# A down projection with seven block products in place of eight in six of its 16 pairs of feature blocks

## The chip, the cores and the metric

One core of one Trainium2 chip runs the whole program in one launch. The metric is the device time of that launch in microseconds (us). An execution counts from its first to its last instruction (the span) and a small remainder around it.

## The reference

The program is a trunk of two layers on 256 tokens of 2048 features, all in float32. Each layer has a token mixer (a retention layer first, block-sparse attention second), a squared-ReLU MLP with 8192 inner features, and a gated embedding. Cut to what matters here:

```python
def rms_norm(x, g):
    y = x * lax.rsqrt(jnp.mean(x * x, axis=-1, keepdims=True) + RMS_EPS)
    return y * g

def sq_relu_mlp(xn, w_up, w_down):
    return jnp.square(jax.nn.relu(xn @ w_up)) @ w_down

for i in range(DEPTH):                       # DEPTH = 2
    h = h + (retention(...) if i == 0 else moba_attention(...))
    h = h + sq_relu_mlp(rms_norm(h, mlp_norm_g[i]), mlp_w_up[i], mlp_w_down[i])
    h = h + per_layer_embed(h, p[i], ...)
return rms_norm(h, final_norm_g)
```

## The kernel before

**Units and pairs.** Every weight matrix is cut on the host into units of 128 partitions x 1024 columns. Two units form a pair of 1 MB, which one transfer of the SP queue brings into a tile `raw` (three buffers). A float32 weight is not multiplied as it is. `conv(i)` splits unit i into a high part `wh` (a rounding cast on ACT, line 221) and a low part `wl` (the rest, `raw - wh`, a subtraction on DVE, line 222), both in the type fp32r, and a product of two split numbers is three matmuls: high x high, high x low, low x high.

**Order.** There is no scheduler; each engine executes its instructions as `run` writes them. For each unit i it issues the load of the pair three pairs ahead, the split of unit i+3 (`LOOK = 3`, four buffers of `wh` and of `wl`), the matmuls of unit i, and then the small tasks that were registered for i with `at(i, ...)`: evacuations of PSUM, norms, transposes. ACT and DVE so run a fixed number of units ahead of PE, and a buffer of `wh` is free for the next split when PE has done with the unit in it.

**The MLP** goes in two halves of 4096 inner features. In an up projection (`phase_a`, names `up0_`, `up1_`) the weights stand still and the 256 tokens of both parts move: a unit is eight matmuls of 512 columns and eight of 256, and two units make a tile of 128 inner features. `evac_up` adds the two halves of the bank (`fold`: a copy `t` on ACT at line 226, an add on DVE at line 227), squares with ReLU (`s2`, line 533) and, one unit later, splits the result into `act[n]` (named `a`). The norm's factor of a token is not in `act`. It comes in at the end, squared, as `r2`, one number for each token.

In a down projection (`project` and `phase_b`, names `dn`) the activations stand still, 128 features x 128 tokens, and 512 weight columns move. For each of four groups of 512 output columns, `c`, the 16 units of a half are gone through; a unit holds two blocks of 128 features and is twelve matmuls, 2 blocks x 2 halves of the tokens x 3. They gather in two of the four PSUM banks of the name `mm`, so that the next group begins in the other two. `evac_dn` adds them, times `r2`, to the residual `h` (line 542). After the second half `finish` squares `h`, transposes it and prepares the operands of what follows. The other banks are two named `y` and two named `aux`.

Of the kernel before, what the change touches and what calls it, by code (L numbers as in the profile page):

```python
# [46 lines left out]
def pack(units):  # L47
    u = units.reshape(-1, 2, P, UC).transpose(0, 2, 1, 3)
    return u
# [10 lines left out]
def cut_b(w):  # L60
    k, n = w.shape
    u = w.reshape(k // 256, 2, P, n // 512, 512).transpose(3, 0, 2, 1, 4)
    return u.reshape(-1, P, UC)


def cut_d(w):
    u = w.reshape(4, 4, P, 2, 2, P).transpose(0, 3, 2, 4, 1, 5)
    return u.reshape(-1, P, UC)


class Core:
    def __init__(self, nc, tc, pools, io):
        self.nc, self.tc, self.io = nc, tc, io
        self.cp, self.wp, self.sp, self.pp = pools
        self.units, self.tasks = [], {}
        self.raws, self.ready = {}, {}


    def unit(self, src, j, mm):
        self.units.append((src, j, mm))  # L80
        return len(self.units) - 1

    def at(self, i, fn):
        self.tasks.setdefault(i, []).append(fn)

    def load(self, i):
        if i >= len(self.units):
            return
        src, j, _ = self.units[i]
        if j % 2:  # L90
            return
        t = self.wp.tile([P, 2, UC], F32, name=f"raw{i}", tag="raw", bufs=3)
        self.nc.sync.dma_start(t, self.io[src][j // 2])
        self.raws[i] = self.raws[i + 1] = t

    def conv(self, i):
        if i >= len(self.units):
            return
        raw = self.raws.pop(i)[:, self.units[i][1] % 2, :]
        wh = self.wp.tile([P, UC], F32R, name=f"wh{i}", tag="wh", bufs=LOOK + 1)  # L100
        wl = self.wp.tile([P, UC], F32R, name=f"wl{i}", tag="wl", bufs=LOOK + 1)
        self.split(wh, wl, raw)
        self.ready[i] = (wh, wl)

    def run(self):
        for fn in self.tasks.pop(-1, []):
            fn()
        for i in range(2, LOOK):
            self.conv(i)
# [29 lines left out]
        return self.sp.tile(list(shape), dt, name=name, tag="s")  # L139

    def small(self, name):
        return self.wp.tile([P, S], F32, name=name, tag="small", bufs=6)


    def mm_a(self, ps, wh, wl, rhs, first, last, turned=False):
# [144 lines left out]
    def stats_b(self):  # L290

        ps = self.aux("rb")
        for t in range(2):
            self.nc.tensor.matmul(ps[:, t * P:(t + 1) * P], self.rn[:, t:t + 1].to_broadcast([P, P]), self.ident, start=True, stop=True)
        self.rb = self.cp.tile([P, S], F32, name="rb", tag="rb", bufs=2)
        self.nc.scalar.copy(self.rb, ps[:, :S])


    def start(self):
        nc, cp, io = self.nc, self.cp, self.io  # L300
        self.g = cp.tile([P, 8, KD], F32, name="g")
        nc.scalar.dma_start(self.g, io["gains"])
        warm = cp.tile([P, 2], F32, name="warm")
        nc.vector.memset(warm, 0.0)
        nc.scalar.activation(warm, warm, AF.Silu)
        self.warm(WARM)
        self.h = [cp.tile([P, 2, 512], F32, name=f"h{c}") for c in range(KD // 4)]
        self.xt = [self.slot("xt", (P, 2, S)) for _ in range(KD // 2)]
        self.raws[0] = self.raws[1] = raw = self.wp.tile([P, 2, UC], F32, name="raw0", tag="raw", bufs=3)
# [12 lines left out]
        load_x(3)  # L322
        self.raws[2] = self.raws[3] = raw2 = self.wp.tile([P, 2, UC], F32, name="raw2", tag="raw", bufs=3)
        for v in range(2):
            dma(raw2[:, v], io["ret_in"][1][:, v])
        load_x(4)
        load_x(5)
        self.load(4)
        load_x(6)
        load_x(7)  # L330
        self.ident = cp.tile([P, P], F32, name="ident")
        dma(self.ident, io["ident"])
        self.cs = cp.tile([P, 2, S], F32, name="cs")
        dma(self.cs, io["cs"])
        self.xx = {}
        wh = self.wp.tile([P, UC], F32R, name="wh0", tag="wh", bufs=LOOK + 1)
        wl = self.wp.tile([P, UC], F32R, name="wl0", tag="wl", bufs=LOOK + 1)
        for n in range(2):
            self.start_x(n)
        for c in (slice(0, 256), slice(256, 512)):  # L340
            self.split(wh[:, c], wl[:, c], raw[:, 0, c])
            if c.start == 0:
                for n in range(2, 4):
                    self.start_x(n)
        self.split(wh[:, 512:], wl[:, 512:], raw[:, 0, 512:])
        self.ready[0] = (wh, wl)
        wh = self.wp.tile([P, UC], F32R, name="wh1", tag="wh", bufs=LOOK + 1)
        wl = self.wp.tile([P, UC], F32R, name="wl1", tag="wl", bufs=LOOK + 1)
        for c in (slice(0, 512), slice(512, 1024)):
            self.split(wh[:, c], wl[:, c], self.raws.pop(1, raw)[:, 1, c])  # L350
        self.ready[1] = (wh, wl)
        for n in range(4, 8):
            self.start_x(n)
# [153 lines left out]
    def natural(self, banks, r):  # L507
# [7 lines left out]
            lo.append(b)  # L515
        return hi, lo

    def mlp(self, layer, gains):
        nc = self.nc
        st = {}  # L520

        def scales():
            self.stats_a()
            st["r2"] = self.cp.tile([P, 2], F32, name="r2", tag="r2", bufs=2)
            nc.vector.tensor_mul(st["r2"], self.rn, self.rn)
        self.at(len(self.units) + 4, scales)
        act = {}
        for half in range(2):
            def evac_up(n, ps, half=half):
                t = self.small("t")  # L530
                self.fold(t, ps)
                s = self.small("s2")
                nc.vector.scalar_tensor_tensor(s, t, 0.0, t, op0=ALU.max, op1=ALU.mult)  # L533
                act[n] = self.slot(f"a{n}", dt=F32R)
                yield
# [3 lines left out]
            def evac_dn(c, banks, i, half=half):  # L539
                for t in range(2):  # L540
                    h = self.h[c][:, t]
                    nc.vector.scalar_tensor_tensor(h, banks[t], st["r2"][:, t:t + 1], h, op0=ALU.mult, op1=ALU.add)  # L542
                if half:
                    self.finish(c, i, gains)
# [53 lines left out]
    def last(self, st, src):  # L598


        nc = self.nc
        per, hold = KD // 2, LOOK + 1
        b = len(self.units)
        fin = {"ssq": {}}

# [214 lines left out]
def program(nc, io):  # L820
    with tile.TileContext(nc) as tc, tc.manual_schedule(), \
            tc.tile_pool(name="const", bufs=1) as cp, tc.tile_pool(name="w", bufs=1) as wp, \
            tc.tile_pool(name="slots", bufs=59) as sp, \
# [12 lines left out]
        c.ple(1, [G_FIN])  # L836
        c.run()
# [63 lines left out]
```

## Time and profile before

| | us |
|---|---|
| median of 3 runs | 2758.9 (2758.51 to 2759.28) |
| span of the profiled execution | 2756.9 |
| PE busy with matmuls | 2743.4 of 2756.9 |
| DVE busy | 1694.6 |
| ACT busy | 1322.8 |

The profiled execution's own time is not listed apart from the three runs; its span is 2.0 us below their median, which is what lies around the span. A busy share is a mean over the program: whether an engine that is at 61% holds up another is read in the stretch in question, from the waits. In the rows, `x4` behind a group is a count, a bracket tells how long the engine had been idle and what ended that, and tile names stand as output`<-`inputs.

### The profile page before, as it was taken

How to read it: one execution, taken by the hardware profiler on the slowest of the kernel's cores; microseconds unless marked ns; L12 is line 12 of the kernel's file. 1: busy time of each engine (PE TensorE's matmuls, PEld its weight loads, DVE VectorE, ACT ScalarE, POOL GpSimd, SP SyncE). 2: the span in 40 equal slices, each digit the busy share in tenths (PEclk: the TensorE clock that was granted, in tenths of full speed). 3: DMA queues.
4: the chain of work that ended last, by engine and by line, in shares of the span. 5: the costliest groups of instructions: out<-in, count | busy, mean ns of one | idle time of the engine just before them, and what ended most of it. 6: DMA issues, size and time to landing. Idle time of an engine off the chain costs nothing.

```text
span 2756.9 us, 34160 instructions
## 1 busy us (share of the span) xinstructions
PE 2743.4 (100%) x13744; PEld 2334.7 (85%) x13744; DVE 1694.6 (61%) x2321; ACT 1322.8 (48%) x1844; POOL 0.2 (0%) x4
## 2 busy tenths in 40 slices
PE   9999999999999999999999999999999999999998
PEld 7888888888888888888888888888888888888886
DVE  6766666655576544665546777775666446664555
ACT  6444444444454433454445555554544334544454
POOL 0000000000000000000000000000000000000000
PEclk9999999999999999999999999999999999999999
DMA  7455555555555555555565555555555555555554
GB/s 277 177 186 186 186 186 186 186 183 186 185 195 186 196 194 190 192 188 192 186 204 188 185 182 179 182 178 185 187 190 192 195 188 196 185 193 189 186 199 153
DMA packets 79450, 522.48 MB, mean 190 GB/s; under 512 B 8987, under 2 KB 12988, under 8 KB 17596
## 3 DMA queue, kind: packets, MB, share of 16 engines
q1 hardware_dynamic: 78476, 519.20, 53.1%
q10 hardware_dynamic: 816, 1.11, 0.3%
q8 instruction: 107, 1.75, 0.3%
q14 instruction: 51, 0.42, 0.0%
HBM read 517.39 MB, written 2.88 MB: 189 GB/s over the span
## 4 chain that ended last, share of the span: by engine, by line
PE 98%; DMA 1%; DVE 0%; ACT 0%; issue 0%; SPq 0%; ACTq 0%; DVEq 0%
PE up L155 17%; PE up L153 9%; PE qk L155 4%; PE aq L155 2%; PE ak L155 2%; PE qk L153 2%; PE aq L153 1%; PE ak L153 1%; PE pu L573 1%; DMA raw<-ret_in 1%; PE xt L255 1%; PE y L461 1%; PE dn__11046 L195 0%; PE dn__20748 L196 0%; PE dn__21353 L197 0%; PE dn__11358 L196 0%
## 5 line engine op out<-in xcount | busy, mean ns | idle before, releaser
L222 DVE TENSOR_TENSOR wl<-raw,wh 128x1024 fp32r<-128x1024 f32 (+1 forms) x971 | 1180.0, 1221 | 652.7 <-ACT wh L221 639.2
L221 ACT CAST wh<-raw 128x1024 fp32r<-128x1024 f32 (+1 forms) x971 | 1013.5, 1048 | 709.3 <-DVE rs_y L278 29.2
L155 PE MATMUL up<-x,wh 128*128 128x512 f32 x2048 | 490.5, 391 | 0.0
L155 PEld LDWEIGHTS up<-x,wh 128*128 128x128 f32 x2048 | 376.1, 188 | 72.4
L153 PEld LDWEIGHTS up<-x,wl 128*128 128x128 f32 x2048 | 263.4, 191 | 10.4
L153 PE MATMUL up<-x,wl 128*128 128x256 f32 x2048 | 266.7, 283 | 0.0
L226 ACT COPY t<-up 128x256 f32<-128x256 f32 x128 | 47.6, 372 | 331.6 <-PE up L155 331.6
L227 DVE TENSOR_TENSOR t<-t,up 128x256 f32<-128x256 f32 x128 | 53.9, 421 | 216.7 <-ACT t L226 216.5
L155 PE MATMUL qk<-x,wh 128*128 128x512 f32 x448 | 109.9, 393 | 0.0
L155 PEld LDWEIGHTS qk<-x,wh 128*128 128x128 f32 x448 | 81.8, 188 | 15.5
L233 ACT ACTIVATE x<-xt,g 128x256 fp32r<-128x256 f32 x112 | 52.5, 478 | 50.6 <-DVE x L234 39.4
L234 DVE SCALAR_TENSOR_TENSOR x<-xt,g,x 128x256 fp32r<-128x256 f32 x112 | 53.0, 481 | 25.7 <-ACT x L233 25.5
L155 PE MATMUL aq<-x,wh 128*128 128x512 f32 x256 | 63.3, 392 | 0.0
L155 PE MATMUL ak<-x,wh 128*128 128x512 f32 x256 | 62.9, 392 | 0.0
L153 PEld LDWEIGHTS qk<-x,wl 128*128 128x128 f32 x448 | 57.4, 191 | 2.2
L153 PE MATMUL qk<-x,wl 128*128 128x256 f32 x448 | 58.1, 283 | 0.0
L533 DVE SCALAR_TENSOR_TENSOR s<-t 128x256 f32<-128x256 f32 x128 | 54.4, 425 | 4.4
L155 PEld LDWEIGHTS ak<-x,wh 128*128 128x128 f32 x256 | 46.7, 189 | 8.7
L155 PEld LDWEIGHTS aq<-x,wh 128*128 128x128 f32 x256 | 46.5, 189 | 8.7
L222 DVE TENSOR_TENSOR a<-s,a 128x256 fp32r<-128x256 f32 x128 | 53.6, 419 | 0.0
L221 ACT CAST a<-s 128x256 fp32r<-128x256 f32 x128 | 52.0, 406 | 0.0
L242 ACT ACTIVATE sq<-h 128x512 f32<-128x512 f32 x48 | 30.1, 628 | 37.5 <-DVE h L542 15.6
(895 smaller groups left out, 4999.3 us busy)
## 6 DMA issues: line engine op xcount, KB each, us to landing
raw<-mlp_up SPq DMA_DIRECT2D x128, 1024.0 KB, 4.8
raw<-mlp_dn SPq DMA_DIRECT2D x128, 1024.0 KB, 4.8
raw<-ret_in SPq DMA_DIRECT2D x94, 1024.0 KB, 4.8
raw<-att SPq DMA_DIRECT2D x48, 1024.0 KB, 4.8
raw<-ret_out SPq DMA_DIRECT2D x32, 1024.0 KB, 4.8
raw<-ple_gate SPq DMA_DIRECT2D x32, 1024.0 KB, 4.8
raw<-att_o SPq DMA_DIRECT2D x16, 1024.0 KB, 4.8
raw<-ple_up SPq DMA_DIRECT2D x4, 1024.0 KB, 4.8
```

Source lines behind the costliest of these rows:

```text
L153: mm(ps[:, S:], wl[:, c], rhs[k][:, :S], start=False, stop=end)
L155: mm(ps, wh[:, c], rhs[k], start=first and k == 0, stop=end)
L221: self.nc.scalar.copy(dst_h, src)
L222: self.nc.vector.tensor_sub(dst_l, src, dst_h.bitcast(F32))
L226: self.nc.scalar.copy(dst, ps[:, :S])
L227: self.nc.vector.tensor_add(dst, dst, ps[:, S:])
L233: self.nc.scalar.activation(t[:, :S], src, AF.Copy, scale=gs)
L234: self.nc.vector.scalar_tensor_tensor(t[:, S:], src, gs, t[:, :S].bitcast(F32), op0=ALU.mult, op1=ALU.subtract)
L242: self.nc.scalar.activation(self.slot("sq"), self.h[c][:, t], AF.Square, accum_out=self.ssq[:, t, c:c + 1])
L255: self.nc.tensor.transpose(ps[:, o * P:(o + 1) * P], self.h[c][:, t, f * P:(f + 1) * P], self.ident)
L461: mm(ys[t], a, w, start=i == 0, stop=i == len(ops) - 1)
L533: nc.vector.scalar_tensor_tensor(s, t, 0.0, t, op0=ALU.max, op1=ALU.mult)
```

## The change

Take a pair of feature blocks a, b of the down projection, the two halves of the tokens, and two groups of 512 output columns. The activations are then a 2 x 2 table of blocks, the weights another, and their product takes eight block products of three matmuls each. The change computes it in seven (Winograd's form of Strassen's method) for the pairs q = 2, 4, 7, 9, 12 and 14 of each 16 (`FAST`), called quick pairs below; the other ten stay as eight products, called plain. It does so in three of the four quarters of each layer's down projection; in the last quarter (second half, last two column groups) `phase_b` stays.

- `sweep` replaces `phase_b` there. It goes through the 16 pairs of a half once for 1024 output columns. The results for 2 token halves x 2 column groups gather in all four `mm` banks, `C00` to `C11`, and the common products of the quick pairs in `P1`, `P5` (the `y` banks) and `P6`, `P7` (the `aux` banks). A plain pair is two units of twelve matmuls. A quick pair is four units, called L, C, M and X here: `low` (6 matmuls), `corner` (3, on 512 columns), `mixed` (6) and `crossed` (6).
- For M and X, DVE first forms differences of weight blocks in place in `raw`, two subtractions of 512 columns each (lines 583, 584, 589 and 590), and then the unit is split as always.
- `combine` forms four sums and differences of the two activation blocks of a quick pair (lines 621 to 624, 128 columns each) and splits them; 24 times in all.
- Since activations of different tokens are now added, the factor `r2` has to be in them: `spread` turns it into rows (two small matmuls and a copy) and `evac_up` multiplies each tile with it (line 638, 128 times). The final add to `h` then has no factor.
- After a sweep `done` adds the four C banks to `h`; one unit later `first` and two units later `second` add the P banks in eight further steps.
- `LOOK` is 4, with five buffers of `wh` and `wl`; during the first twelve units of the program the split still runs three ahead (`SOON`). `raw` keeps three buffers; a load is issued at a pair's first unit. There are 62 slots for 59 and 8 small tiles for 6.

```diff
-LOOK = 3
+LOOK = 4
+SOON = 3
+HOLD = 4
+FAST = [q in (2, 4, 7, 9, 12, 14) for q in range(16)]
...
     def run(self):
...
         for i in range(len(self.units)):
-            self.load(i + 6)
-            self.conv(i + LOOK)
+            self.load(self.units[i][0] + 3)
+            while done <= i + (SOON if i < 12 else LOOK):
+                self.conv(done)
+                done += 1
             wh, wl = self.ready.pop(i)
             self.units[i][2](wh, wl)
...
+    def sweep(self, name, src, first, fast, x, done):
...
+            if quick:
+                plan += [(q, self.low, [("C01", (q, "S4"), 0), ("C00", (b, 0), 1)]),
+                         (q, self.corner, [("P1", (a, 0), 0)]),
+                         (q, self.mixed, [("P5", (q, "S1"), 0), ("P7", (q, "S3"), 1)]),
+                         (q, self.crossed, [("P6", (q, "S2"), 0), ("C10", (b, 1), 1)])]
+            else:
+                plan += [(q, lambda raw: self.halves(raw[:, 0]), plain(a, False)),
+                         (q, lambda raw: self.halves(raw[:, 1]), plain(b, True))]
...
+    def mixed(self, raw):
+        v, r = self.nc.vector, raw[:, 0]
+        v.tensor_sub(r[:, :512], r[:, 512:], r[:, :512])
+        v.tensor_sub(r[:, 512:], raw[:, 1, :512], r[:, 512:])
+        return self.halves(r)
+
+    def crossed(self, raw):
+        v, r = self.nc.vector, raw[:, 1]
+        v.tensor_sub(r[:, :512], r[:, :512], raw[:, 0, :512])
+        v.tensor_sub(r[:, 512:], r[:, 512:], r[:, :512])
+        return self.halves(r)
...
+        def combine(q, a, b):
...
+            v.tensor_add(s1, a[:, P:], b[:, P:])
+            v.tensor_sub(s2, s1, a[:, :P])
+            v.tensor_sub(s3, a[:, :P], a[:, P:])
+            v.tensor_sub(s4, b[:, :P], s2)
+            self.split(h, l, f)
...
+                v.tensor_mul(s, s, st["rb"])
                 self.split(act[n][:, :S], act[n][:, S:], s)
+                if FAST[n // 2]:
...
+            def done(banks, i, g, half=half):
+                h = [self.h[2 * g], self.h[2 * g + 1]]
+                for bank in ("C00", "C10", "C01", "C11"):
+                    t, c = int(bank[1]), int(bank[2])
+                    v.tensor_add(h[c][:, t], h[c][:, t], banks[bank])
...
+                self.at(i + 1, first)
+                self.at(i + 2, second)
...
-            self.project(f"dn{half}_", f"mlp_dn{layer}", half * 64, FH // 256, lambda k: act[k], evac_dn)
+            for g in range(2):
+                if half and g:
+                    for c in (2, 3):
+                        e = len(self.units) + n - 1
+                        self.phase_b(f"dn{c}_", src, (4 + c) * n, n, lambda k: act[k], lambda banks, c=c, e=e: evac_dn(c, banks, e))
+                else:
+                    self.sweep(f"dn{half}{g}_", src, (half * 2 + g) * n, FAST, x, lambda banks, i, g=g, done=done: done(banks, i, g))
```

What stands on DVE for the first pairs of the first down projection, before: one subtraction of 1024 columns for each unit, two for each tile `raw`.

```order
L222 TENSOR_TENSOR wl326_7776<-raw326_7719,wh326_7775 128x1024
L222 TENSOR_TENSOR wl327_7794<-raw326_7719,wh327_7793 128x1024
L222 TENSOR_TENSOR wl328_7810<-raw328_7757,wh328_7809 128x1024
L222 TENSOR_TENSOR wl329_7828<-raw328_7757,wh329_7827 128x1024
L222 TENSOR_TENSOR wl330_7844<-raw330_7791,wh330_7843 128x1024
L222 TENSOR_TENSOR wl331_7862<-raw330_7791,wh331_7861 128x1024
```

The same engine in the changed kernel, at the quick pair q = 4 of that projection (`raw164`) and the first unit of the plain pair behind it:

```order
L238 TENSOR_TENSOR wl_7913<-raw164_7854,wh_7912 128x1024
L238 TENSOR_TENSOR wl_7925<-raw164_7854,wh_7924 128x512
L583 TENSOR_TENSOR raw164_7854<-raw164_7854 128x512
L584 TENSOR_TENSOR raw164_7854<-raw164_7854 128x512
L238 TENSOR_TENSOR wl_7940<-raw164_7854,wh_7939 128x1024
L589 TENSOR_TENSOR raw164_7854<-raw164_7854 128x512
L590 TENSOR_TENSOR raw164_7854<-raw164_7854 128x512
L238 TENSOR_TENSOR wl_7958<-raw164_7854,wh_7957 128x1024
L238 TENSOR_TENSOR wl_7976<-raw165_7892,wh_7975 128x1024
```

A quick pair has eight rows where a pair had two, and the splits of M and X stand behind the differences from which they are made.

Where a group of columns ends in the first down projection, DVE had this before (`dn0_0_0`, `dn0_0_1` are its two banks; the next group was by then in two others):

```order
L222 TENSOR_TENSOR wl337_7964<-raw336_7893,wh337_7963 128x1024
L222 TENSOR_TENSOR wl338_7980<-raw338_7927,wh338_7979 128x1024
L542 SCALAR_TENSOR_TENSOR h0_89<-dn0_0_0__7725,r2_6197,h0_89 128x512
L542 SCALAR_TENSOR_TENSOR h0_89<-dn0_0_1__7726,r2_6197,h0_89 128x512
L222 TENSOR_TENSOR wl339_8000<-raw338_7927,wh339_7999 128x1024
```

At the end of the first sweep it now has this (`raw177` is the second pair of the next sweep, `raw178` its first quick pair):

```order
L238 TENSOR_TENSOR wl_8391<-raw177_8349,wh_8390 128x1024
L238 TENSOR_TENSOR wl_8407<-raw177_8349,wh_8406 128x1024
L651 TENSOR_TENSOR h0_89<-h0_89,dn00_C00__7819 128x512
L651 TENSOR_TENSOR h0_89<-h0_89,dn00_C10__7823 128x512
L651 TENSOR_TENSOR h1_90<-h1_90,dn00_C01__7827 128x512
L651 TENSOR_TENSOR h1_90<-h1_90,dn00_C11__7831 128x512
L238 TENSOR_TENSOR wl_8429<-raw178_8388,wh_8428 128x1024
L657 TENSOR_TENSOR h0_89<-h0_89,q_8448 128x512
L658 TENSOR_TENSOR q_8448<-q_8448,dn00_P6__7928 128x512
L659 TENSOR_TENSOR u_8449<-q_8448,dn00_P5__7916 128x512
L238 TENSOR_TENSOR wl_8455<-raw178_8388,wh_8454 128x512
```

All four C banks, in which the next sweep begins at once, are emptied behind the split of a pair two pairs ahead, and the P banks between the splits of the next quick pair.

More of the change, by code (lines that the diff above doesn't have):

```diff
@@ L74, in __init__, with part @@
         self.cp, self.wp, self.sp, self.pp = pools
-        self.units, self.tasks = [], {}
+        self.units, self.pairs, self.tasks = [], [], {}
         self.raws, self.ready = {}, {}
     def unit(self, src, j, mm):
-        self.units.append((src, j, mm))
+        return self.part(src, j // 2, lambda raw: self.halves(raw[:, j % 2]), mm)
+    def part(self, src, pair, conv, mm):
+        if not self.pairs or self.pairs[-1] != (src, pair):
+            self.pairs.append((src, pair))
+        self.units.append((len(self.pairs) - 1, conv, mm))
         return len(self.units) - 1
@@ L84, in at, with load, operand, halves @@
         self.tasks.setdefault(i, []).append(fn)
-    def load(self, i):
-        if i >= len(self.units):
+    def load(self, q):
+        if q >= len(self.pairs) or q in self.raws:
             return
[L89 to L94, printed above, removed]
-    def conv(self, i):
[L97 to L103, printed above, removed]
+        src, pair = self.pairs[q]
+        t = self.raws[q] = self.wp.tile([P, 2, UC], F32, name=f"raw{q}", tag="raw", bufs=3)
+        self.nc.sync.dma_start(t, self.io[src][pair])
+    def operand(self, cols=UC):
+        return [self.wp.tile([P, cols], F32R, name=f"w{n}", tag=f"w{n}", bufs=LOOK + 1) for n in "hl"]
+    def halves(self, raw):
+        wh, wl = self.operand(raw.shape[-1])
+        self.split(wh, wl, raw)
+        return wh, wl
+    def conv(self, i):
+        if i < len(self.units):
+            q, conv, _ = self.units[i]
+            self.ready[i] = conv(self.raws[q])
     def run(self):
@@ L516, in natural, with plain, mm @@
         return hi, lo
+    def sweep(self, name, src, first, fast, x, done):
+        plan, banks, seen = [], {}, {}
+        tags = {"P1": "y", "P5": "y", "P6": "aux", "P7": "aux"}
+        cut = (slice(0, 512), slice(512, 1024))
+        def plain(k, second):
+            cols = (1, 0) if second else (0, 1)
+            order = (1, 0) if second else (0, 1)
+            return [(f"C{t}{cols[j]}", (k, t), j) for j in order for t in range(2)]
+        for q, quick in enumerate(fast):
+            a, b = 2 * q, 2 * q + 1
+            if quick:
[6 more added lines that the diff above has]
+                         (q, lambda raw: self.halves(raw[:, 1]), plain(b, True))]
+        for n, (_, _, ops) in enumerate(plan):
+            for m, (bank, _, _) in enumerate(ops):
+                seen.setdefault(bank, []).append((n, m))
+        for n, (q, conv, ops) in enumerate(plan):
+            def mm(wh, wl, n=n, ops=ops):
+                m = self.nc.tensor.matmul
+                for i, (bank, which, j) in enumerate(ops):
+                    start, stop = (n, i) == seen[bank][0], (n, i) == seen[bank][-1]
+                    if start:
+                        banks[bank] = self.bank(f"{name}{bank}_", *((tags[bank], 2) if bank in tags else ()))
+                    ps, (xh, xl), c = banks[bank], x(*which), cut[j]
+                    m(ps, xh, wh[:, c], start=start, stop=False)
+                    m(ps, xh, wl[:, c], start=False, stop=False)
+                    m(ps, xl, wh[:, c], start=False, stop=stop)
+            i = self.part(src, first + q, conv, mm)
+        self.at(i, lambda: done(banks, i))
@@ new lines, in low, with corner @@
+    def low(self, raw):
+        return self.halves(raw[:, 1])
+    def corner(self, raw):
+        return self.halves(raw[:, 0, :512])
+    def mixed(self, raw):
[8 more added lines that the diff above has]
+        return self.halves(r)
@@ L524, in scales, with rows, x, evac_up @@
             st["r2"] = self.cp.tile([P, 2], F32, name="r2", tag="r2", bufs=2)
-            nc.vector.tensor_mul(st["r2"], self.rn, self.rn)
-        self.at(len(self.units) + 4, scales)
-        act = {}
+            v.tensor_mul(st["r2"], self.rn, self.rn)
+        def rows():
+            st["rb"] = self.spread(st["r2"])
+        self.at(b + 4, scales)
+        self.at(b + 6, rows)
+        act, sums = {}, {}
+        def x(k, t):
+            if isinstance(t, str):
+                h, l = sums[k]
+                c = slice((int(t[1]) - 1) * P, int(t[1]) * P)
+                return h[:, c], l[:, c]
+            return act[k][:, t * P:(t + 1) * P], act[k][:, S + t * P:S + (t + 1) * P]
+        def combine(q, a, b):
+            f = self.slot("sf")
+            h, l = self.slot("sh", dt=F32R), self.slot("sl", dt=F32R)
+            s1, s2, s3, s4 = (f[:, i * P:(i + 1) * P] for i in range(4))
+            v.tensor_add(s1, a[:, P:], b[:, P:])
[3 more added lines that the diff above has]
+            self.split(h, l, f)
+            sums[q] = h, l
         for half in range(2):
-            def evac_up(n, ps, half=half):
+            held = {}
+            def evac_up(n, ps, half=half, held=held):
                 t = self.small("t")
@@ L532, in evac_up @@
                 s = self.small("s2")
[L533 removed]
+                v.scalar_tensor_tensor(s, t, 0.0, t, op0=ALU.max, op1=ALU.mult)
                 act[n] = self.slot(f"a{n}", dt=F32R)
[L535 removed]
+                for _ in range(4 if half == 0 and n < LEAD else 1):
+                    yield
+                v.tensor_mul(s, s, st["rb"])
                 self.split(act[n][:, :S], act[n][:, S:], s)
[L537 removed]
```

68 lines of the change are left out of this document (49 added, 19 removed).

## The prediction

> **What bounds the kernel now.** I read the page's busy times and its chain first, then the waits of PE, a stretch of one down projection, and one unit of it in order of time.
>
> ```profile
> PE 2743.4 (100%) x13744; PEld 2334.7 (85%) x13744; DVE 1694.6 (61%) x2321; ACT 1322.8 (48%) x1844; POOL 0.2 (0%) x4
> PEclk9999999999999999999999999999999999999999
> PE 98%; DMA 1%; DVE 0%; ACT 0%; issue 0%; SPq 0%; ACTq 0%; DVEq 0%
> ```
>
> PE is busy throughout, its granted clock is full, and 98% of the chain that ends last is PE. The waits of PE, over the whole program:
>
> ```profile
> PE warm L364 <- DVE zero L357: 1.5, 1, 1.5
> PE qk L182 <- ACT wh L221: 0.8, 2, 0.4
> ```
>
> Both lie in the first microseconds. So a matmul removed is worth its full time as long as nothing makes PE wait, and any wait added is paid in full. What a down projection leaves free on the other engines (first half of layer 0, all four column groups):
>
> ```profile
> core 0: us, PE busy (x) PEld busy (x) DVE busy (x) ACT busy (x) POOL busy (x), PEclk, DMA share, GB/s
> 924.60:1098.60 174.00, 174.00 (x769) 144.14 (x768) 83.66 (x74) 68.02 (x66) 0.00 (x0) 1.00 0.55 193
> ```
>
> DVE is at half. One unit, where two column groups meet:
>
> ```profile
> 1006.24 0.39 PE L195 MATMUL dn__8003<-wh,a 128*128 128x512 f32 x1
> ...
> 1006.44 1.05 ACT L221 CAST wh<-raw 128x1024 fp32r<-128x1024 f32 x1 [1.67 <-PE dn__8004 L197]
> ...
> 1007.52 1.23 DVE L222 TENSOR_TENSOR wl<-raw,wh 128x1024 fp32r<-128x1024 f32 x1 [1.50 <-ACT wh L221]
> ...
> 1008.78 0.33 SPq L93 DMA_DIRECT2D raw<-mlp_dn  x1
> ...
> 1008.96 0.39 PE L195 MATMUL dn__8003<-wh,a 128*128 128x512 f32 x1
> ...
> 1010.24 1.23 DVE L222 TENSOR_TENSOR wl<-raw,wh 128x1024 fp32r<-128x1024 f32 x1 [1.49 <-ACT wh L221]
> ...
> 1011.38 0.74 DVE L542 SCALAR_TENSOR_TENSOR h<-dn__8003,r,h 128x512 f32<-128x512 f32 x1
> ...
> 1012.04 0.74 DVE L542 SCALAR_TENSOR_TENSOR h<-dn__8004,r,h 128x512 f32<-128x512 f32 x1
> ```
>
> These rows give the prices. Twelve matmuls take PE 1008.96 - 1006.24 = 2.72, so one is 0.2267. A cast lets its DVE step begin 1.08 later. A 1024-column DVE step holds DVE for 1.14 (1010.24 to 1011.38) and ends after 1.23. An add out of PSUM holds it for 0.66 and ends after 0.74. The load that reuses a `raw` tile goes out 0.03 after that tile's last `wl` (1007.52 + 1.23 = 8.75). The rotation of a retention head shows 512-column steps and a chain from DVE to ACT and back:
>
> ```profile
> 523.82 0.68 DVE L379 TENSOR_TENSOR kc<-kr,cs 128x512 f32<-128x512 f32 x1
> ...
> 524.42 0.69 DVE L380 TENSOR_TENSOR ks<-kr,cs 128x512 f32<-128x512 f32 x1
> 525.14 0.42 DVE L381 TENSOR_TENSOR kr<-kc,ks 128x256 f32<-128x256 f32 x1
> 525.48 0.42 DVE L382 TENSOR_TENSOR kr<-kc,ks 128x256 f32<-128x256 f32 x1
> 525.93 0.62 ACT L221 CAST kh<-kr 128x512 fp32r<-128x512 f32 x1 [3.29 <-DVE kr L382]
> ...
> 526.59 0.69 DVE L222 TENSOR_TENSOR kl<-kr,kh 128x512 fp32r<-128x512 f32 x1 [0.69 <-ACT kh L221]
> ```
>
> A 512-column step is followed after 0.60 by one that does not need it, after 0.72 by one that does; a cast follows its source's end by 0.03.
>
> **What is removed and added on PE.** Three matmuls for each quick pair, 6 pairs, 3 sweeps, 2 layers: 108 x 0.2267 = 24.5 us less. `spread` adds two small matmuls in each layer; the same two stood in the attention:
>
> ```profile
> 1576.58 0.61 PE L294 MATMUL rb<-ident,rn 128*128 128x128 f32 x4
> 1576.94 1.20 PE L153 MATMUL ak<-x,wl 128*128 128x256 f32 x8
> ```
>
> They displaced what follows by 0.36, so 0.7 in all. PE did not wait for them there, two units behind the same norm; I add nothing.
>
> **The splits of a quick pair.** In order: L 1.14; C 0.72 (the first difference overwrites what it reads); two differences 0.72 each; the cast 1.08; M 1.14; two differences 0.72 each; the cast 1.08; X 1.14. Sum 9.18 us, in which DVE idles during both casts, since nothing stands between in its order. PE needs 21 x 0.2267 = 4.76 for that pair. A plain pair is 2.28 against 5.44. A sweep of 16 comes to 6 x 9.18 + 10 x 2.28 = 77.9 on this chain and 83.0 on PE, so on average it hides. What decides is how far ahead it may run: four units, which are 10.9 us of plain units but 4.76 of a quick pair, and three `raw` tiles.
>
> **The loop through `raw`.** The tile of q = 4 is reused by q = 7, and its last reader is X of q = 4.
>
> ```profile
> raw<-mlp_dn SPq DMA_DIRECT2D x128, 1024.0 KB, 4.8
> DMA to landing us min/median/max: 4.6/4.8/11.0
> ```
>
> From the end of that step to the end of X of q = 9: issue 0.03, landing 4.8, cast 1.08, q = 7 9.18, q = 8 2.28, q = 9 9.18, end 0.09: 26.64. The splits of q = 5 and 6 fit into the landing. PE takes 2 x 4.76 + 3 x 5.44 = 25.84 from X to X. Each turn of this loop therefore makes PE wait 0.8, at X of 9 and again at X of 14.
>
> **The end of a sweep.** No group can begin in two other banks any more: the next stage's first product needs the bank of C00. Its add stands behind the split of the pair two ahead, whose `raw` tile is that of q = 14. From the end of X(14)'s `wl`: 0.03 + 4.8 + 1.08 + 1.14 + 1.14 + 0.74 = 8.9. PE starts X about 0.2 before that end (only its second matmul reads `wl`) and is through with X and q = 15 after 1.36 + 5.44, at 6.6. Wait 2.3, after each of six sweeps. What follows, sweep, up projection or `phase_b`, is held alike.
>
> **The second sweep of each layer** follows a sweep directly. When PE starts, DVE still has three adds (2.0), L of q = 2 (1.14), `first` (2.2), C (0.6), `second` (3.5) and M and X (7.4 with their casts): X is ready after 16.7, from PE's side 16.5; PE wants it after 4 x 2.72 + 3.4 = 14.3. Wait 2.2. Then q = 3 and 4 are 2.28 + 9.18 = 11.5 on the chain and 10.2 on PE: another 1.3.
>
> **The up projections.** The last tile's evacuation, before:
>
> ```profile
> 919.27 0.37 ACT L226 COPY t<-up 128x256 f32<-128x256 f32 x1 [2.66 <-PE up L155]
> 919.54 1.06 ACT L221 CAST wh<-raw 128x1024 fp32r<-128x1024 f32 x1
> 919.67 0.42 DVE L227 TENSOR_TENSOR t<-t,up 128x256 f32<-128x256 f32 x1 [1.80 <-ACT t L226]
> 920.13 0.42 DVE L533 SCALAR_TENSOR_TENSOR s<-t 128x256 f32<-128x256 f32 x1
> 920.59 0.41 ACT L221 CAST a<-s 128x256 fp32r<-128x256 f32 x1
> 920.63 1.23 DVE L222 TENSOR_TENSOR wl<-raw,wh 128x1024 fp32r<-128x1024 f32 x1
> 921.13 1.05 ACT L221 CAST wh<-raw 128x1024 fp32r<-128x1024 f32 x1
> 921.77 0.42 DVE L222 TENSOR_TENSOR a<-s,a 128x256 fp32r<-128x256 f32 x1
> ```
>
> DVE idles 1.80 in each tile's 5.57, which takes the new multiplication (0.42). `combine` falls on six of the 32 tiles: four steps of 0.3, a cast, a split of 512, about 2.7 with its waits; the four units' lead bears that. But the combination of q = 14 stands just ahead of the last two splits and the last tile's add. Laid out from these rows that add ends 3.2 after the sweep's start, and C11 needs its bank after nine matmuls, 2.0. Wait 1.2, at the two sweeps of each layer that follow an up projection.
>
> **Sum.** Waits in a layer: first and third sweep 1.2 + 0.8 + 0.8 + 2.3 = 5.1 each, second 2.2 + 1.3 + 0.8 + 0.8 + 2.3 = 7.4, together 17.6; in two layers 35.2. Against the profiled execution's 2756.9: - 24.5 + 0.7 + 35.2 = + 11.4, a span of 2768.3; with the 2.0 by which the median of the runs lies above it, **2770**. The wider window elsewhere gives nothing, as PE waits nowhere; SP issues as many loads in the same order, each behind the last reader of its tile.
>
> Ends: the 0.72 steps at 0.60, the row without dependence, take 1.2 from the loop. The waits inside the sweeps go, the others shrink by about 0.4, and 20 remain: 2755. A landing 1 us later (most land at 4.8, one took 11.0) puts 1 on each of three waits of a sweep, 18 in all: 2788. I take the dependent row, since each of these steps reads or overwrites its forerunner's data.
>
> **Rivals.** (1) Faster: the loop is shorter than PE's 25.84 by s. Then X of 14 comes s early, and the wait at a sweep's end is 2.3 - s. With the other waits (4 x 1.2 + 2 x 3.5 = 11.8) the total is 25.6 - 6s, under the 23.8 that the matmuls give back from s = 0.3, and worth 0.2% from s = 1.2; at s = 2.3 it is 2747. For it: DVE is at half today, and no row shows this chain repeated. Against: it needs 3 us less than rows add up to.
>
> (2) The same time: s near 0.4, the end at 2755 above.
>
> (3) Landings 1 us late, 2788. Against: the loads in the loop go out alone, some 9 us behind the one before.
>
> (4) After each wait at a sweep's end PE runs slowly, as at the start of the program:
>
> ```profile
> 1.48 3.74 PE L364 MATMUL warm<-zero 128*128 128x512 f32 x9 [1.48 <-DVE zero L357]
> ```
>
> Nine matmuls took 3.74 there, 0.42 each. If six times nine ran so, that costs 54 x 0.19 = 10 us: 2780. Against: the waits are 2.3 long at most, the clock row is full everywhere, and no idle time of that length stands in this trace behind its start. The Trainium skill (TensorE: Matmul & The Clock Gate, section "Why this matters for your kernels") asks for no idle gap above about 3 us between bursts, or the clock halves; by that rule these waits pass, if no two run together.
>
> **How the numbers follow.** Forecast 0.45 (2764 to 2778), rival 1 0.22, rival 2 0.20, rivals 3 and 4 together 0.13. A measurement here can tell 0.2% from no change, 5.5 us. Faster is rival 1, the same is rival 2, slower the rest, 0.58. The range 2746 to 2788 leaves out half of rival 1 and what lies beyond 3.
>
> **What would show it.** Right: PE waits for `wl` of `raw` at X of q = 9 and 14 by under 1 us, for line 651 at each sweep's end by about 2, and most at the first quick pair of the second sweep; the down projections have 108 matmuls fewer. Wrong: no wait on line 651 (then the end of the sweep was misjudged), an L that does not wait for its load, or a granted clock below 1.00 behind the waits.

## The result, and the profile after

The changed kernel takes 2783.97 us, the median of four runs (2782.08 to 2788.04), against 2758.7 before: a ratio of 1.0094 (1.008 to 1.0108). It is 25 us slower; 11 were forecast. The profiled execution took 2782.08, its span is 2780.3, which is 1.8 less.

The page's busy times, clock row and chain, after:

```profile
PE 2736.0 (98%) x13644; PEld 2316.2 (83%) x13644; DVE 1949.6 (70%) x2833; ACT 1365.0 (49%) x1948; POOL 0.2 (0%) x4
...
PEclk9999999999999999999999999999999999999999
...
PE 77%; DVE 13%; ACT 5%; DMA 3%; issue 2%; ACTq 0%; SPq 0%
```

PE has the hundred matmuls fewer (108 removed, 8 for `spread`). Yet the chain that was 98% PE is now 77% PE, and DVE, ACT and the loads hold a fifth of it. PE's waits (what waits, for whom, us in total, times, longest):

```profile
PE up L171 <- DVE h L651: 4.2, 2, 2.1
PE dn_P__18937 L570 <- DVE wl L238: 3.0, 4, 0.8
...
PE dn_C__18820 L569 <- DVE h L651: 2.3, 1, 2.3
PE dn_C__18219 L569 <- DVE t L243: 2.2, 1, 2.2
PE dn__11392 L211 <- DVE h L651: 2.1, 1, 2.1
...
PE dn_P__7928 L570 <- DVE wl L238: 1.5, 2, 0.8
...
PE dn_C__10791 L569 <- DVE t L243: 0.9, 1, 0.9
```

Line 651 is `done`: the ends of the sweeps, as forecast over 2 us each. `wl` L238 of a `dn_P` bank is X. Line 243 is the add that empties the bank of an up projection's last tile; C11 needs that bank. So each forecast wait is there, in its place; the sizes differ. The end of the first sweep, where two splits that wait for a load stand ahead of the first add:

```profile
1010.86 2.00 ACT L237 CAST wh<-raw 128x1024 fp32r<-128x1024 f32 x2 [2.28 <-DMA raw<-mlp_dn]
...
1011.94 2.36 DVE L238 TENSOR_TENSOR wl<-raw,wh 128x1024 fp32r<-128x1024 f32 x2 [1.37 <-ACT wh L237]
...
1014.22 0.68 DVE L651 TENSOR_TENSOR h<-h,dn_C__7819 128x512 f32<-128x512 f32 x1
...
1015.05 0.47 PE L569 MATMUL dn_C__8432<-wh,a 128*128 128x512 f32 x1 [2.08 <-DVE h L651]
```

One turn of the loop through `raw` in the order of time, from the load that X of q = 4 releases to the one that X of q = 9 releases:

```profile
951.43 0.33 SPq L105 DMA_DIRECT2D raw<-mlp_dn  x1
...
960.05 0.69 DVE L584 TENSOR_TENSOR raw<-raw 128x512 f32<-128x512 f32 x1
961.13 1.05 ACT L237 CAST wh<-raw 128x1024 fp32r<-128x1024 f32 x1 [3.18 <-PE dn_C__7831 L571]
962.22 1.22 DVE L238 TENSOR_TENSOR wl<-raw,wh 128x1024 fp32r<-128x1024 f32 x1 [1.48 <-ACT wh L237]
...
964.08 0.69 DVE L590 TENSOR_TENSOR raw<-raw 128x512 f32<-128x512 f32 x1
964.88 2.95 ACT L237 CAST wh<-raw 128x1024 fp32r<-128x1024 f32 x3 [2.70 <-DVE raw L590]
...
978.85 0.33 SPq L105 DMA_DIRECT2D raw<-mlp_dn  x1
```

The turn is 978.85 - 951.43 = 27.42, where 26.64 was laid out. A cast that follows a difference starts 0.11 after its end (964.08 + 0.69 to 964.88), not 0.03, three times in a turn; M's cast of q = 7 starts 0.39 after its difference (960.05 + 0.69 to 961.13), 0.36 more than laid out, as it waits for a `wh` buffer that PE still reads; the load and the cast behind it take 0.15 more.

The stretch around the start of the second sweep in layer 0 (1012.5 on) and of that in layer 1 (2218.5 on), with the granted clock (third number from the right):

```profile
1012.50:1015.80 3.30, 1.22 (x6) 0.71 (x5) 3.30 (x5) 1.89 (x3) 0.00 (x0) 1.00 0.92 340
1015.80:1019.20 3.40, 3.40 (x10) 2.60 (x9) 3.33 (x6) 0.00 (x0) 0.00 (x0) 0.52 0.70 289
1019.20:1022.60 3.40, 3.40 (x16) 2.85 (x15) 2.93 (x5) 0.62 (x1) 0.00 (x0) 0.97 0.00 0
2218.50:2221.80 3.30, 1.05 (x6) 0.58 (x4) 3.11 (x4) 1.68 (x3) 0.00 (x0) 1.00 0.93 355
2221.80:2225.20 3.40, 3.40 (x15) 2.81 (x16) 3.38 (x5) 1.32 (x3) 0.00 (x0) 1.00 0.96 342
```

After a wait of 2.1 PE ran at half clock for 3.4 us in the first place, ten matmuls for fifteen; after a wait of 2.3 in the second it did not. The page's clock row, in slices of 70 us, shows none of it. It happened behind three of this run's eight waits above 2 us (the last matmul before to the first after: 2.4 to 2.6).

### The profile page after: what moved, and what is told of

Its sections match the earlier page's. It is cut to its first block, busy times and chain, and to the rows that moved or that the text cites. A ratio compares the mean times of both kernels' runs of the same rounds, so it can differ in the third digit from the quotient of the medians.

```text
span 2780.3 us, 35119 instructions
## 1 busy us (share of the span) xinstructions
PE 2736.0 (98%) x13644; PEld 2316.2 (83%) x13644; DVE 1949.6 (70%) x2833; ACT 1365.0 (49%) x1948; POOL 0.2 (0%) x4
## 3 DMA queue, kind: packets, MB, share of 16 engines
q8 instruction: 107, 1.75, 0.2%
## 4 chain that ended last, share of the span: by engine, by line
PE 77%; DVE 13%; ACT 5%; DMA 3%; issue 2%; ACTq 0%; SPq 0%
PE up L171 12%; DVE wl L238 8%; PE up L169 6%; ACT wh L237 5%; PE qk L171 4%; PE aq L171 2%; PE ak L171 2%; DMA raw<-mlp_dn 2%; PE qk L169 2%; PE aq L169 1%; PE ak L169 1%; PE pu L714 1%; DVE raw L590 1%; DVE raw L584 1%; PE xt L271 1%
## 5 line engine op out<-in xcount | busy, mean ns | idle before, releaser
L238 DVE TENSOR_TENSOR wl<-raw,wh 128x1024 fp32r<-128x1024 f32 (+1 forms) x1043 | 1233.3, 1201 | 542.2 <-ACT wh L237 536.4
L237 ACT CAST wh<-raw 128x1024 fp32r<-128x1024 f32 (+1 forms) x1043 | 1055.7, 1031 | 648.7 <-DVE raw L584 102.9
L238 DVE TENSOR_TENSOR a<-s,a 128x256 fp32r<-128x256 f32 x128 | 54.5, 426 | 60.5 <-ACT a L237 60.5
L638 DVE TENSOR_TENSOR s<-s,rb 128x256 f32<-128x256 f32 x128 | 53.5, 418 | 0.0
```

The lines of the kernel that those rows point to most:

```text
L237: self.nc.scalar.copy(dst_h, src)
L238: self.nc.vector.tensor_sub(dst_l, src, dst_h.bitcast(F32))
L638: v.tensor_mul(s, s, st["rb"])
```

## The experiments

The account to test, theory A: the lost time is PE waiting for splits that come late, since a quick pair hands over between VectorE and ScalarE again and again in a fixed order, and the lead of four units and three `raw` tiles doesn't cover that. Its rival, theory B: the new form itself costs (the sweep, the scaling ahead, or DVE's volume of new steps). All times stand against the kernel before on the same chip, 2758.6 to 2758.9 each time.

**No quick pairs.** The sweeps, scaled activations and the wider window without the seven products.

```diff
-FAST = [q in (2, 4, 7, 9, 12, 14) for q in range(16)]
+FAST = [False] * 16
...
-                self.at(i + 1, first)
-                self.at(i + 2, second)
+                if any(FAST):
+                    self.at(i + 1, first)
+                    self.at(i + 2, second)
+                elif half:
+                    self.at(i + 2, last)      # finish alone
```

> All 16 pairs are plain: the sweep over four banks, the scaling of the activations ahead of the down projection and the wider window stay; no seven-product pair, no combination of activations, no differences. Theory A (the time is lost because a quick pair's splits hand over between VectorE and ScalarE too often, and the four-unit lead and three raw tiles can't cover that): no wait at X, none above 0.5 us at a sweep's end, so the time of before plus the two matmuls of spread in each layer: 2759 to 2763. Theory B (the form of the sweep, the scaling ahead, or the volume of new steps at the entry costs in itself): 2768 or more, with waits of 1 to 2 us at the entry of the sweeps and on line 651 at their ends.

Measured: 2763.52, ratio 1.0017 (1.0008 to 1.0026), just above A's range and far from B's. All that is left of the waits inside the MLP:

```profile
PE up L171 <- DVE h L651: 0.7, 2, 0.4
...
PE dn__11088 L211 <- DVE h L651: 0.4, 1, 0.4
PE dn_C__18393 L569 <- DVE h L651: 0.4, 1, 0.4
```

The form costs 4.8: 0.9 for `spread` (an up projection went from 179.07 to 179.52, twice), six ends of some 0.6 each in the spaces between the starts of PE's matmuls, restart included, and small gaps. Neither entries nor X wait. The changed kernel also sets `dynamic_dma_scratch_size=1024`, which the section on the change doesn't name; this run has it too, so it is within the 4.8.

**The matmuls alone.** M and X use the splits of the raw blocks, so that DVE and ACT do no more than for a plain pair. The four differences and the splits behind them are left out, and the results are not the reference's.

```diff
     def low(self, raw):
-        return self.halves(raw[:, 1])
+        self.low_w = self.halves(raw[:, 1])
+        return self.low_w
     def corner(self, raw):
-        return self.halves(raw[:, 0, :512])
+        self.top_w = self.halves(raw[:, 0])
+        return self.top_w
     def mixed(self, raw):
-        ... (two differences)
-        return self.halves(r)
+        return self.top_w
     def crossed(self, raw):
-        ... (two differences)
-        return self.halves(r)
+        return self.low_w
```

> Quick pairs issue their seven products, but VectorE and ScalarE split the raw blocks as for a plain pair (two splits of 1024 columns, taken twice): the four differences and the splits behind them are left out, so the numbers aren't the reference's. The combinations of activations stay. Theory A: the 108 matmuls bring their 24.5 us and only the entry waits stay (about 2.3 in first halves, 1.1 in second ones, 7 together): 2740 to 2747. Theory B (the seven-product order on PE, its banks or the sweep is itself dearer): 2760 or more, with gaps on PE that no split explains.

Measured: 2747.53, ratio 0.9963 (0.9949 to 0.9976). The waits at X are gone, the ends are back at 0.4, the entries stay (2.1, 2.1, 0.9, 0.9). The seven products themselves are not dear on PE. It lies 0.5 above A's range, which had counted only the entries: the six ends take some 3.7 us in the spaces between PE's starts, and a stretch at half clock behind one entry 1.7.

**The differences together.** The same steps in another order.

```diff
     def mixed(self, raw):
         v.tensor_sub(r[:, :512], r[:, 512:], r[:, :512])
         v.tensor_sub(r[:, 512:], raw[:, 1, :512], r[:, 512:])
+        x = raw[:, 1]
+        v.tensor_sub(x[:, :512], x[:, :512], r[:, :512])
+        v.tensor_sub(x[:, 512:], x[:, 512:], x[:, :512])
         return self.halves(r)
     def crossed(self, raw):
-        ... (the same two differences)
         return self.halves(raw[:, 1])
```

> The same instructions in another order: all four differences of a quick pair stand one behind the other, ahead of M's split, so M's cast lies beside the last two differences and X's cast beside M's split. VectorE's volume is unchanged; the chain of a quick pair falls from 9.18 to about 7.0, the loop through raw from 27.4 to about 23, under PE's 25.84. Theory A: the 12 waits at X (1.36 each, 16) go, those at the sweeps' ends (6 x 2.3) nearly go, as X of 14 comes over 2 us earlier, those in the second sweep too (5); entry waits of 7 stay, and some stretches at half clock with them: 2743 to 2755. Rival (VectorE's volume of work in quick pairs, not its order, makes PE wait): 2780 to 2788, as the changed kernel. A middle value, 2765 to 2772, would say that the X waits go but the sweeps' ends don't.

Measured: 2748.55, ratio 0.9962 (0.995 to 0.9975). DVE's work is all there, 1956.8 us busy, and no X is waited for:

```profile
PE 2724.4 (99%) x13644; PEld 2315.2 (84%) x13644; DVE 1956.8 (71%) x2833; ACT 1376.3 (50%) x1948; POOL 0.2 (0%) x4
```

```profile
959.92 0.69 DVE L584 TENSOR_TENSOR raw<-raw 128x512 f32<-128x512 f32 x1
960.65 0.69 DVE L586 TENSOR_TENSOR raw<-raw 128x512 f32<-128x512 f32 x1
961.01 1.05 ACT L237 CAST wh<-raw 128x1024 fp32r<-128x1024 f32 x1 [2.57 <-DVE raw L584]
961.38 0.69 DVE L587 TENSOR_TENSOR raw<-raw 128x512 f32<-128x512 f32 x1
962.09 1.23 DVE L238 TENSOR_TENSOR wl<-raw,wh 128x1024 fp32r<-128x1024 f32 x1
```

M's cast (961.01) now lies beside X's differences, and `wl` follows them without an idle moment. The sweeps' ends are down to 0.4, one to 1.0; the entries wait as before, with a stretch at half clock behind one of them. The rival in volume falls: 35 us between two orders of the same instructions.

**The adds first.** At a sweep's end the four adds go ahead of the two splits of the pair two ahead.

```diff
...
+            if i not in self.ends and i + 1 not in self.ends:
+                ahead()                       # the splits up to LOOK units ahead
             wh, wl = self.ready.pop(i)
             self.units[i][2](wh, wl)
             for fn in self.tasks.pop(i, []):
                 fn()
+            if i in self.ends:
+                ahead()
```

> At the end of a sweep the four adds that empty the C banks are issued ahead of the two splits of the pair two ahead, which wait for a load; all else as changed. Theory A: the six waits on line 651 (2.3 each, 14) shrink to under 0.5, the 12 waits at X stay, the half-clock stretches behind sweep ends (1.6 each, one or two in a run) go: 2764 to 2771. Rival (the adds come late for another reason, or what is gained at the end is given back at the first quick pair, since its splits now start later): 2778 to 2785, with the wait moved to L or X of q = 2.

Measured: 2773.23, ratio 1.0053 (1.0041 to 1.0066), between the two. The six waits on the adds went, 13.6 us, but new ones came:

```profile
PE xt L277 <- DVE h L672: 2.0, 2, 1.0
...
PE dn_P__8549 L575 <- ACT wh L243: 1.0, 1, 1.0
PE dn_P__18937 L575 <- ACT wh L243: 1.0, 1, 1.0
```

The quick pairs, the second sweep's first above all, wait 3.3 us longer in sum, and the transposes behind the last sweep 1.0 twice: 5.3 of the 13.6 are given back. The rival was right by that part.

**Five pairs, farther apart.** The changed kernel's own order of splits.

```diff
-FAST = [q in (2, 4, 7, 9, 12, 14) for q in range(16)]
+FAST = [q in (3, 5, 8, 10, 13) for q in range(16)]
```

> The changed kernel's order of splits, but five quick pairs per sweep (3, 5, 8, 10, 13) in place of six (2, 4, 7, 9, 12, 14): 90 matmuls fewer than before, 20.4 us. Theory A (what counts is whether the loop through three raw tiles, two quick chains and a plain pair, is longer than PE's time for it; here no loop through raw holds two quick pairs and a plain one from q to q + 5 with the same distance, as each pair of neighbours is followed by two plain pairs): waits at X in the second sweep of a layer and at entries only, about 2 to 6 a layer: 2746 to 2754. Rival (each quick pair costs its share of the loss whatever its place): five sixths of the changed kernel's loss: 2776 to 2782.

Measured: 2750.65, ratio 0.9971 (0.996 to 0.9982). One X in each sweep waits, with its restart 1.2, 7.0 in all, and no entry does:

```profile
PE dn_P__18908 L570 <- DVE wl L238: 0.8, 1, 0.8
PE dn_P__10886 L570 <- DVE wl L238: 0.8, 1, 0.8
```

One pair less and another spacing turn 25 us of loss into 8 of gain: the cost does not go with the number of quick pairs. The time lies in A's range, but the waits are not where A put them (second sweeps and entries), so that agreement is partly luck.

**A late combination.** With the differences together, the combination for q = 14 is put off into the sweep.

```diff
-                        yield
+                        for _ in range(6 if n == 29 else 1):
+                            yield
                         combine(n // 2, held.pop(n - 1), held.pop(n))
```

> The four differences together, as before, and the combination of the activations of q = 14 (the last before a sweep) is issued five units later, inside the sweep. Theory A (the entry wait is the last tile's evacuation standing behind that combination): the four entry waits (2.2, 2.1, 0.9, 0.9, each with about 0.1 more for the restart) go to under 0.3, no half-clock stretch is left behind them: 2739 to 2743. Rival (the entry wait comes of the scaling ahead, which every tile has): no change, 2746 to 2750, with the wait on line 243 as long as it was.

Measured: 2739.13, ratio 0.9929 (0.9917 to 0.9942). No wait on line 243 is left, and no stretch at half clock behind the start of the program.

**All three, and with one split put off in place of two.** Differences together, the late combination and the adds first; in the second of the two runs the condition of the adds' order is only `if i not in self.ends`.

> Differences together, the late combination and the adds at a sweep's end ahead of the splits. Theory A: the six waits of 0.4 on line 651 go too (with the restart 0.5 each, 3 in all): 2736 to 2740. Rival (the later splits make PE wait at the next sweep's first quick pair, or the transposes behind the last sweep come late by 1.0): as without it, 2740 to 2744.

> As all three, but at a sweep's end only the second split of the pair two ahead stands behind the four adds, the first one ahead of them as in the changed kernel. Theory A (VectorE is about 1.3 us late at the next sweep's first quick pair when two splits are put off; one split less is half of that): the six waits of 0.4 at the ends go, and those at X of the second sweep and at the transposes shrink below 0.5: 2736 to 2739. Rival (the adds themselves wait for PE's last matmuls and hold the splits up alike): 2739 to 2741.

With two splits put off: 2739.77, ratio 0.9932 (0.9919 to 0.9946), no better than without. The number lies in A's range, but it is the rival that came: the ends' waits went, and others of 0.9 and 1.0 took their place:

```profile
PE xt L277 <- DVE h L673: 2.0, 2, 1.0
...
PE dn_P__18925 L576 <- DVE wl L244: 0.9, 1, 0.9
```

With one: 2736.41, ratio 0.9919 (0.9905 to 0.9933), the fastest here, and its whole list of waits is

```profile
PE warm L390 <- DVE zero L383: 1.5, 1, 1.5
```

From 2758.9, less 24.5 for the matmuls, plus 0.9 for `spread`, comes 2735.3. The change's promise is there once nothing waits. A seventh pair or a fourth `raw` tile wasn't tried.

**What half clock hangs on.** The kernel before, with chains put into each layer's MLP that stop PE:

```diff
+        def probe(k):
+            d = self.cp.tile([P, S], F32, name="pd", tag="pd", bufs=1)
+            ps = self.aux("pa")
+            nc.tensor.matmul(ps[:, :P], self.ident, self.ident, start=True, stop=True)
+            nc.vector.tensor_copy(d[:, :P], ps[:, :P])
+            for _ in range(k):
+                nc.vector.tensor_scalar_mul(d[:, :P], d[:, :P], 1.0)
+            ps = self.aux("pb")
+            nc.tensor.matmul(ps[:, :P], d[:, :P], self.ident, start=True, stop=True)
+        for j in range(30):
+            self.at(len(self.units) + 12 + 6 * j, lambda j=j: probe((0, 4, 2, 6, 3, 8, 5, 1, 10, 7)[j % 10]))
```

> The kernel before with 30 chains put into each layer's MLP, six units apart: a small matmul, 1 to 11 VectorE steps on its result, a small matmul on theirs, so that PE is idle for some 0.6 to 5 us each time. The question is what the half-speed stretches of the changed kernel hang on (3 of its 9 waits of 2.2 to 2.5 us had one behind them, none of its 14 waits of 1.0 us). Theory A (the wait itself, by its length): none behind waits under 2, some behind those of 2 to 3, all behind longer ones, each about 3.4 us long at 0.43 a matmul, costing 1.4 to 1.7. Rival (they come of something else, such as where a wait falls in a fixed period): half speed behind short waits too, and full speed behind some above 4.

The trace of the changed kernel has eight waits above 2 us, not nine. Measured: 2927.92 in one run, from start to start of the matmuls around a wait 0.66 to 3.37 us. None of the 30 waits up to 1.8 had half clock behind it; of those of 2.06 one in six, of 2.32 three, of 2.58 four, of 2.84 three, of 3.37 all six. All but one of the 17 stretches cost 1.4 to 1.7 us (40 matmuls of a down projection took 10.54 for 8.93); the one, behind a wait of 3.37, lasted 5.3 and cost 2.6. Two waits of one down projection, the shorter with half clock behind it, the longer without:

```profile
1030.50:1032.91 2.41, 0.37 (x3) 0.21 (x2) 1.80 (x8) 1.04 (x1) 0.00 (x0) 1.00 0.64 187
1032.91:1036.31 3.40, 3.40 (x11) 2.76 (x12) 0.99 (x1) 0.00 (x0) 0.00 (x0) 0.66 0.43 176
1069.30:1072.44 3.14, 0.58 (x4) 0.37 (x3) 2.25 (x10) 1.04 (x1) 0.00 (x0) 1.00 0.65 203
1072.44:1075.84 3.40, 3.40 (x16) 2.85 (x17) 0.99 (x1) 0.14 (x1) 0.00 (x0) 1.00 0.29 120
```

This is what theory A forecast, none under 2, some up to 3, all above; but in between length alone does not decide. The ends of the slow stretches lie on a fixed grid of 3.413 us, each within 0.25 of it. Counted by that grid, and with 0.2 taken off each wait for the small matmul before it, the first wait has 2.1 idle in one period; the second is cut into 1.6 and 1.1. With over 1.9 idle in a period, half clock followed each time (16 of 16); with under 1.75, never. In between lie five waits at 1.85 to 1.86, one of them with half clock.

The same with short waits close together:

```diff
-            self.at(len(self.units) + 12 + 6 * j, lambda j=j: probe((0, 4, 2, 6, 3, 8, 5, 1, 10, 7)[j % 10]))
+            for k in ((3, 3), (4,), (2, 2), (3, 3), (2, 2, 2), (3,))[j % 6]:
+                self.at(len(self.units) + 12 + 6 * j, lambda k=k: probe(k))
```

> The kernel before with waits of PE, as in the run with 30 chains a layer, but set close together: single ones of 1.8 and 1.5 us from start to start, two of 1.5, two of 1.3, three of 1.3, with two small matmuls between the waits of a group. In the run with single waits half speed followed where over 1.9 us of idle fell into one period of 3.413 us, and never behind a wait of 1.8 or less. Theory A (idle time is added up within a period): none behind the single ones, half speed behind some of the pairs (two of 1.3 hold about 2.1 idle in all, two of 1.5 about 2.6) and most of the triples. Rival (a single idle stretch of over 1.9 is needed): full speed behind all of them.

Measured: 2997.83 in one run. Behind the 20 single waits of 1.5 and 1.8: never. Behind three of 1.27: 10 of 10. Behind two of 1.27: 8 of 10. Behind two of 1.5, too long together for one period: 4 of 20. A triple (with the stretch that follows), and a single wait of 1.8:

```profile
985.50:992.00 6.50, 3.50 (x20) 2.78 (x19) 3.92 (x11) 1.04 (x1) 0.00 (x0) 1.00 0.45 161
992.00:995.40 3.40, 3.40 (x11) 2.65 (x10) 0.54 (x1) 0.00 (x0) 0.00 (x0) 0.57 0.02 5
1046.50:1050.26 3.76, 2.24 (x11) 1.72 (x10) 2.57 (x7) 1.43 (x2) 0.00 (x0) 1.00 0.33 94
1050.26:1053.66 3.40, 3.40 (x16) 2.87 (x17) 0.99 (x1) 0.15 (x1) 0.00 (x0) 1.00 0.56 236
```

Idle time is added up within a period: with a grid of 3.4134 and a bound between 1.74 and 1.81 all 60 groups are told apart. The phase of the grid and the bound were fitted to the same 60 groups. That PE counts as idle during the small matmuls of a group does not fit: two of 1.5 would then be one wait of 3.5, and behind single ones of 3.37 half clock came six times in six.

By this count the two runs' bounds differ, as four of the five waits at 1.85 to 1.86 in the first run had no half clock. Counted from start to start, nothing taken off, one bound of 2.06 to 2.08 tells 119 of the 120 groups of both runs apart, again fitted to the same groups. The changed kernel's trace, which was not in that fit, agrees: its slow stretches end 27.1 and 328.0 periods of 3.4134 from the first, and by the grid through these ends (0.06 earlier, as in the fit) the three waits with half clock behind them have 2.2 to 2.6 in one period, four others 1.6 at most, and the fifth, 2.1, lies at the bound.

## Why the prediction was right or wrong

Right: the sign, each place of a wait, the rows that would show it, and the worth of a removed matmul. Two steps failed above all. The loop through `raw` was laid out too short, so that its 12 waits at X came to 14.7 for 9.6; and half clock behind the waits was put at nothing and left to rival 4, where it took 4.7. The entries, 2.0 short, and the restarts, put at nothing, add the rest. In the profiled run, from the spaces between the starts of PE's matmuls (X and the second sweep with the restart of 0.1 behind each wait; the restarts of the ends and entries are in the other gaps):

| term | forecast | measured |
|---|---|---|
| matmuls removed | -24.5 | -24.5 |
| `spread` | 0.7 | 0.9 |
| X of q = 9 and 14, 12 waits | 9.6 | 14.7 |
| sweep ends, 6 | 13.8 | 13.6 |
| second sweep, q = 2 and 4 | 7.0 | 5.4 |
| entries, 4 | 4.8 | 6.8 |
| half clock, 3 stretches | 0 | 4.7 |
| other gaps, restarts among them | 0 | 2.6 |
| sum | 11.4 | 24.2 |

The measured sum puts the span at 2756.9 + 24.2 = 2781.1; it is 2780.3, as the program's start, up to the first up projection, was 0.8 shorter than before (743.3 for 744.1).

- **The loop through `raw`.** Its 26.64 was 0.78 short. "A cast follows its source's end by 0.03" came from one row; behind the 66 differences that a cast waits for in this trace it is 0.11. Their 512 columns are not the reason, since other steps of 512 columns are followed after 0.03, here line 677:

```profile
1466.20 0.68 DVE L677 TENSOR_TENSOR h<-h,dn__11746 128x512 f32<-128x512 f32 x1
...
1466.91 0.63 ACT L258 ACTIVATE sq<-h 128x512 f32<-128x512 f32 x1 [1.89 <-DVE h L677]
```

What differs in the trace is that each of those 66 casts waits for three semaphores and has an event-semaphore instruction ahead of it, one that does no work of its own but wait; this one has none. That it is the reason was not tested. No term stood for a cast that waits for a `wh` buffer. As the loop stood only 0.8 above PE's 25.84, 3% of its length nearly doubled the excess, to 1.58 in this turn. Over the 12 waits 1.2 in the mean show at X for the 0.8, restarts included. That the order is the cause is shown by the differences together: no wait at X is left.
- **The ends.** 2.3 forecast, 2.2 to 2.4 measured. This was the best term. Its cause, the add behind the split that waits for a load, is confirmed by the adds first. That some 0.4 would be left even without quick pairs was not seen: the split behind which the add stands needs the `wh` buffer that PE has just left (in the run without quick pairs the cast starts at 1010.42 on PE's release, the subtraction at 1011.51, the add at 1012.65).
- **The entries.** 1.2 for all four was a mean of two sorts: 2.1 and 2.2 in first halves, 0.9 in second ones. The cause, the combination of q = 14, is confirmed by the late combination.
- **The second sweep.** 2.2 in layer 0 and 3.2 in layer 1, for 3.5 each. Layer 0 alone has a half-clock stretch in front, which gave DVE 1.6 more to catch up; that this is the reason was not tested.
- **Rival 4.** The prediction held the waits too short for it, and cited the Trainium skill, page "TensorE: Matmul & The Clock Gate", section "Why this matters for your kernels", for a bound of about 3 us. The measurement decides: half clock came behind waits of 2.1 and 2.2 in this kernel, and behind 11 of the 24 waits of 2.06 to 2.84 in the probe. (This kernel's 2.1 and 2.2 are listed idle times; counted from start to start, like the probe's, they are 2.4 to 2.6.) It happened three times for 1.6 rather than six for 1.7. The prediction named a granted clock below 1.00 as a sign against it, and this is 4.7 of the 12.8 that its sum lacked.
- **Rivals 1 and 2** needed a loop shorter than PE's time. The kernel with the differences together is that case, and there the time fell as rival 1 says: 2748.55, against 2747 worked out for the loop 2.3 shorter. The close number is luck in part: rival 1 kept 7.0 for the second sweeps, which went, and had nothing for the ends' 0.4 to 1.0 and the half clock, which came.
- **Rival 3**, later landings, did not come: `raw<-mlp_dn` landed after 4.9 in the median, for 4.8.

## What to carry to other kernels

Before arithmetic is moved from PE to the splits, lay out one turn of the tightest loop, from a buffer's release to its next, on the engines that hand over to each other in it; shares of busy time (70% here) don't show it, and a turn that comes out within a few per cent of PE's time has to be taken as late. Where two engines work in turn on the same tiles, write the steps that need no answer together, so that one engine's answer falls beside the other's next step: that alone was 35 us here. Work that isn't needed soon doesn't belong ahead of what releases a PSUM bank.

## What the runs showed of the hardware

- PE's clock follows fixed periods of 3.413 us, as fitted to the ends of 39 slow stretches in two runs. Where over some 2.06 us of waiting, from start to start, fell into one period, also as a sum of shorter waits, about one period at half clock followed, and mostly cost 1.6. A wait of 2.1 to 2.3 as the profile lists it therefore cost 1.6 more or nothing, by where it fell. In the four runs of the changed kernel the listed mean clock falls from 0.997 to 0.995 as the time rises from 2782 to 2788; that the number of such stretches makes this difference is likely, not shown. The Trainium skill, page "TensorE: Matmul & The Clock Gate", section "What's actually happening", gives a free-running window of 3413 ns; the fitted period agrees with that, while the row of its table that asks for an idle window of about 3.4 us does not.
- A wait of PE cost more than the idle time that the profile lists for it: 0.16 more, as the profile ends a matmul 0.39 after its start where the next one can start after 0.2267, and another 0.08 to 0.11, as the matmul behind the wait held the next one up for 0.31 to 0.34 (0.341 at X, 0.307 at a sweep's end).
- A ScalarE step that waits for a VectorE step started 0.03 to 0.04 after the end that the profile gives for it in all 338 cases of the changed kernel's trace without an event-semaphore instruction ahead, and 0.08 to 0.11 after it in 75 of 82 cases with one.
